# Squares' pieces in the rows' tiles, and norms spread by two transfers

## The chip, the cores and the metric

The kernel runs on one core of a Trainium2 chip. The metric is device time in microseconds of one execution, as the median of several runs. The core has a matrix engine (TensorE, PE in the profile; its weight loads are PEld), VectorE (DVE), ScalarE (ACT), GpSimd (POOL) and a queue engine (SyncE, SP) that issues nearly all transfers of this kernel, in one order.

## The reference

One layer of an encoder for two groups of tokens, 1024 of `x_sample` and 256 of `x_prompt`, 2048 features each:

```
hn   = rms_norm(x, norm_g)                      # x / sqrt(mean(x^2) + eps) * g
proj = hn @ w_in
...                                             # a state space part, a windowed attention,
...                                             # and an attention over 256 memory rows
mk, mv = split(rms_norm(mem, mem_norm_g) @ w_mem_kv)
return x + concat([o_ssd, o_att, o_mem]) @ w_out
```

What matters here is `rms_norm(x)`: for each of the 1280 tokens one number, 1/sqrt(mean of squares + eps), by which all 2048 features of that token are multiplied.

## The kernel before

**Products.** All large products are in float32, each operand split into a high half and a low half (`wh`, `wl` of the weights, `xH`, `xL` of the rows), and computed as three passes: high by high, high by low, low by high (lines 254 to 256, 289 to 291, 1199 to 1201). A weight tile is loaded into `wraw` (four buffers), ScalarE rounds it to `wh`, and VectorE subtracts to get `wl` (three buffers each; `wsplit`, lines 202 and 203). A block runs over 16 rounds, one for each 128 input features; a round has three passes for each of its four or five token tiles. Some weights are multiplied by a scheme of seven products for four (`block_pair`, `seven`), whose row sums lie in tiles tagged `tH0` to `tH7` and `tL0` to `tL7` of the pool `fin`.

**Order.** The 1280 tokens are ten tiles of 128: group 0 has tiles 0 to 4, group 1 tiles 5 to 9. The program begins with the two blocks of the memory rows (`mk`, then `mv`, four token tiles each), which need no norms of `x`. Then come the q block of group 0, ten units of the seven products, the blocks kv, mq, z0 and z1 of group 0, and then group 1. Beside the blocks run two lanes of small steps, written as generators: every round of a block advances each lane by a given number of steps (`pump`, with rates such as `MR[0]` = 1.75 for lane 0 in the memory blocks, from round 8 of the first). A step's instructions on ScalarE and VectorE are held behind the weight split that was traced last (`marks`). Within such limits a scheduler puts each engine's instructions in order by priority and by when it takes their inputs and buffers to be free, so a load may be issued long before the place where it is traced.

**Squares and norms.** `x_stats(0)` is in lane 0 beside the memory blocks. It takes the five token tiles of group 0 in twenty pieces of 128 x 512. A piece (`xst`) is loaded four steps ahead, ScalarE squares it and adds up its rows (line 1336), after four pieces VectorE adds the four sums, and GpSimd makes the power -1/2 (lines 120 and 121). The result is one column of `rx` per token tile: a number for each token, one token per partition. The pieces lie in the tiles tagged `evt` and `evu` of the pool `ev`, two buffers each, in which the tiles of the blocks' results (`mkr`, line 415) also lie. `x_stats(1)` does the same for tiles 8 and 9 beside the kv block, in other tiles; tiles 5 to 7 are done in between (`stage_stats`).

**Spreading the norms.** The rows are held with features on the partitions and tokens along the row, so the norms are needed along the row, the same on all 128 partitions: `rbc`, 128 x 640. `x_rows(grp)` makes it. It multiplies a broadcast column of `rx` by the identity, which gives a tile with the column turned into each of 128 rows, five times, into the PSUM tile `prx`, and VectorE copies the result to `rbc` (lines 1392 to 1397). In the profile each of the five products appears as two passes. The readers of `rbc` are `p_fill` (line 1234), which makes the rows of group 0 from round 9 of the `mv` block on, and `fill_direct` with `norm=True` (line 190), which makes those of group 1. The step of round 9 first asks that `x_rows(0)` be finished.

Of the kernel before, what the change touches and what calls it, by code (L numbers as in the profile page):

```python
# [10 lines left out]
F32 = mybir.dt.float32  # L11
# [8 lines left out]
P = 128  # L20
# [23 lines left out]
def hymba_encoder_kernel(  # L44
# [7 lines left out]
    V, A, G, T, S = nc.vector, nc.scalar, nc.gpsimd, nc.tensor, nc.sync  # L52
# [3 lines left out]
    def xrow(t):  # L56
        return x_sample[t * P:(t + 1) * P] if t < NS else x_prompt[(t - NS) * P:(t - NS + 1) * P]
# [8 lines left out]
    ev = ctx.enter_context(tc.tile_pool(name="ev", bufs=2))  # L66
# [4 lines left out]
    fin = early.enter_context(tc.tile_pool(name="early", bufs=1))  # L71
# [4 lines left out]
    def const(shape, name, dtype=F32):  # L76
        return cp.tile(shape, dtype, tag=name, name=name)
# [4 lines left out]
    def psum(name):  # L82
        return mix.tile([P, 512], F32, tag="mix", name=name)
# [3 lines left out]
    ident = identr.bitcast(F32)  # L87
# [11 lines left out]
    rx = const([P, 14], "rx")  # L99
    rbc = const([P, 640], "rbc")  # L100
    carry = const([P, 12, 4], "carry")
    def dram(shape, name):
        return dr.tile(shape, F32, tag=name, name=name)
# [8 lines left out]
    yp_d = [dram([P, 1024], f"yp_{t}") for t in range(NT)]  # L112
    sb_d = [dram([P, 1024], f"sb_{t}") for t in range(NT)]
    mk_d = dram([P, 4, 256], "mk_d")
    ac_d = [dram([160, P], f"ac_{g}") for g in range(2)]
    mr_d = [dram([P, 512], f"mr_{i}") for i in range(4)]
    mv_d = dram([P, 4, 512], "mv_d")
# [1142 lines left out]
    def p_step(j):  # L1260
        if j == 9:
            need(x_rows, [0])
        with ExitStack() as st:
            for ins in marks:
                st.enter_context(tc.issue_after(ins))
            if j in (25, 27):
                weight_sums(w_in_pairs, (j - 25) // 2)
            for f, k in sorted(p_plan.get(j, ()), key=lambda x: ((p_split, p_sums, p_fill, p_load).index(x[0]), x[1])):
                f(k)
# [53 lines left out]
    def stats(tiles, place, ahead=4, group=None):  # L1323

        n = 4 * len(tiles)
        group = group or n
        pieces, s4 = {}, None
        for g in range(0, n, group):
            m = min(group, n - g)
            for i in range(m + ahead):  # L1330
                if i >= ahead:
                    t, c = divmod(g + i - ahead, 4)
                    if c == 0:
                        s4 = sm.tile([P, 4], F32, tag="s4", name="xs4", bufs=4)
                    x = pieces.pop(g + i - ahead)
                    A.activation(x, x, AF.Square, accum_out=s4[:, c:c + 1])
                    if c == 3:
                        r = rx[:, tiles[t][1]:tiles[t][1] + 1]
                        V.reduce_sum(out=r, in_=s4, axis=AX.X)
                        rsqrt(r, r, 1.0 / D, 1)  # L1340
                if i < m:
                    t, c = divmod(g + i, 4)
                    pieces[g + i] = place(i)
                    with tc.issue_after(last_load[0].ins):
                        S.dma_start(pieces[g + i], tiles[t][0][:, c * 512:c * 512 + 512])
                yield

    def x_stats(grp):
        if grp == 0:
            yield from stats([(xrow(t), t) for t in range(5)],  # L1350
                             lambda i: ev.tile([P, 512], F32, tag="evt" if i % 2 else "evu", name="xst"))
        else:
            yield from stats([(xrow(t), t) for t in (8, 9)],
                             lambda i: mp.tile([P, 512], F32, tag="xs" if i % 2 else "ya", name="xst", bufs=2))
# [33 lines left out]
    def x_rows(grp):  # L1388

        yield  # L1390
        yield
        for o, n in ((0, 4), (4, 1)):
            ps = psum("prx")
            for i in range(n):
                t = 5 * grp + o + i
                T.matmul(ps[:, i * P:(i + 1) * P], rx[:, t:t + 1].broadcast_to([P, P]), ident, start=True, stop=True)
            V.tensor_copy(rbc[:, o * P:(o + n) * P], ps[:, :n * P])
        yield

    def refill_x(grp):  # L1400
        def f(q):
            need(x_rows, [grp])
            return [part(fill_direct, q, j, x_turned[grp, (4 * q + j) * P:(4 * q + j + 1) * P, :],
                         gain=vec[:, R_G + 4 * q + j:R_G + 4 * q + j + 1], norm=True) for j in range(4)]
        return f
# [60 lines left out]
    w_mk = w_mem_rows(0)  # L1466
    pend.extend(first[1:] + [u for q in range(1, 4) for u in refill_mem(q)])
    queue(0, x_stats, [0])
    queue(0, x_rows, [0])
    run(block_tok(w_mk, 4, ev_mk, places=TURNED), MR[0], hold=8)  # L1470
    V.tensor_scalar(out=vec[:, R_CB:], in0=vec[:, R_CB:], scalar1=0.5, scalar2=None, op0=ALU.mult)
# [54 lines left out]
    queue(0, mk_prep, range(4))  # L1526
    queue(0, mem_values, [0])
    queue(1, x_stats, [1])
    queue(1, x_rows, [1])
    w_kv = w_in_rows("kv")  # L1530
# [57 lines left out]
    for c in range(2, 4):  # L1588
        j0 = 16 * (c - 3)
        for k in block_tok(w_out_rows(c), 5, ev_out(c * 512), before_last=lambda _: beside_step(j0 + 14)):  # L1590
            if j0 + k == -7:
# [5 lines left out]
                fin = ctx.enter_context(tc.tile_pool(name="fin", bufs=2))  # L1597
# [83 lines left out]
```

## Time and profile before

| | us |
|---|---|
| Median of 3 runs (1801.31 to 1802.7) | 1802.39 |
| The profiled execution's time | 1802.42 |
| Its span, first to last instruction | 1800.7 |
| TensorE busy | 1791.2 (99%) |
| VectorE busy | 1244.3 (69%) |
| ScalarE busy | 903.0 (50%) |
| GpSimd busy | 439.5 (24%) |
| Granted TensorE clock | 1.000 |

Busy time of TensorE is the union of its passes. Passes overlap in the records, so the distance between the starts of two passes tells more than their length. A row of a stretch in order of time gives start, length, engine, line, operation, tiles, shape and count; in brackets stands the idle time before it and what ended it. A row of waits gives who waited for whom: total us, times, longest.

### The profile page before, as it was taken

To read this page: it belongs to the slowest core of one execution; us is meant where nothing else is said; L and a number is where in the kernel's file an instruction comes from. 1 tells how busy PE (TensorE), PEld (TensorE's weight loads), DVE (VectorE), ACT (ScalarE), POOL (GpSimd) and SP (SyncE) were. 2 spreads that over 40 slices of the span, in tenths; PEclk is the share of its full clock that TensorE was granted. 3 is DMA by queue.
4 is the path that set the end of the run, shared out by engine and by line. 5 is a ranking of instruction groups with operands and counts; after the bars stand their busy time and mean duration, and the time that the engine had idled before them with its cause. 6 is when DMAs were issued, how large, how long until landed. Compare 5 with 4: busy or idle time off the path is not lost.

```text
span 1800.7 us, 30423 instructions
## 1 busy us (share of the span) xinstructions
PE 1791.2 (99%) x10546; PEld 1606.1 (89%) x10546; DVE 1244.3 (69%) x2422; ACT 903.0 (50%) x2039; POOL 439.5 (24%) x714
## 2 busy tenths in 40 slices
PE   9999999999999999999999999999999999999999
PEld 7789999999887899999989987887898888889999
DVE  5595788877657978775755866666885654866665
ACT  6554455444445756564435646544574533543332
POOL 0105789961110000000000000001100000058775
PEclk9999999999999999999999999999999999999999
DMA  8664455446544644444436355457785564644442
GB/s 291 198 179 120 138 153 146 129 136 218 164 136 147 184 134 140 121 132 134 119 96 192 110 161 180 128 178 235 231 266 168 184 190 138 216 153 147 142 143 80
DMA packets 198891, 290.58 MB, mean 161 GB/s; under 512 B 18960, under 2 KB 80464, under 8 KB 198736
## 3 DMA queue, kind: packets, MB, share of 16 engines
q1 hardware_dynamic: 198592, 288.57, 52.7%
q8 instruction: 83, 1.36, 0.3%
q14 instruction: 72, 0.59, 0.1%
q10 hardware_dynamic: 144, 0.06, 0.0%
HBM read 231.12 MB, written 57.44 MB: 160 GB/s over the span
## 4 chain that ended last, share of the span: by engine, by line
PE 61%; DVE 1%; ACT 1%; issue 1%; DMA 1%; POOL 0%; POOLq 0%; ACTq 0%; DVEq 0%
PE acc L254 9%; PE acc L256 8%; PE acc L255 8%; PE acc L289 5%; PE acc L291 5%; PE acc L290 5%; PE acc L1199 3%; PE acc L1201 3%; PE acc L1200 3%; PE py L931 2%; PE po L674 1%; PE ppt L664 1%; PE accm L1200 1%; PE accm L1201 1%; PE accm L1199 1%
## 5 line engine op out<-in xcount | busy, mean ns | idle before, releaser
L203 DVE TENSOR_TENSOR wl<-wraw,wh 128x512 fp32r<-128x512 f32 (+1 forms) x480 | 338.9, 708 | 241.3 <-ACT wh L202 230.7
L254 PE MATMUL acc<-wh,xH 128*128 128x512 f32 (+1 forms) x1248 | 481.9, 386 | 0.2 <-ACT mkr L416 0.2
L255 PE MATMUL acc<-wl,xH 128*128 128x512 f32 (+1 forms) x1248 | 472.2, 378 | 0.9 <-DVE wl L203 0.6
L256 PE MATMUL acc<-wh,xL 128*128 128x512 f32 (+1 forms) x1248 | 472.8, 379 | 0.0
L202 ACT ACTIVATE wh<-wraw 128x512 fp32r<-128x512 f32 (+1 forms) x480 | 292.4, 613 | 323.5 <-PE acc L256 173.3
L254 PEld LDWEIGHTS acc<-wh,xH 128*128 128x128 f32 x1248 | 234.5, 188 | 45.1 <-issue 4.8
L255 PEld LDWEIGHTS acc<-wl,xH 128*128 128x128 f32 x1248 | 234.7, 188 | 43.8 <-DVE wl L203 3.3
L256 PEld LDWEIGHTS acc<-wh,xL 128*128 128x128 f32 x1248 | 234.2, 188 | 43.9 <-issue 0.9
L289 PE MATMUL acc<-xH,wh 128*128 128x320 f32 x640 | 204.5, 320 | 0.0
L291 PE MATMUL acc<-xH,wl 128*128 128x320 f32 x640 | 198.6, 310 | 0.0
L290 PE MATMUL acc<-xL,wh 128*128 128x320 f32 x640 | 198.3, 310 | 0.0
L203 DVE TENSOR_TENSOR sl<-ws,sh 128x384 fp32r<-128x384 f32 x144 | 99.6, 695 | 96.9 <-ACT sh L202 96.6
L202 ACT ACTIVATE sh<-ws 128x384 fp32r<-128x384 f32 x144 | 74.6, 523 | 176.5 <-POOL ws L1171 81.5
L1171 POOL TENSOR_TENSOR ws<-wraw 128x128 f32<-128x128 f32 x144 | 91.1, 633 | 202.0 <-DMA wraw<-in_w_in_pairs_dram 83.6
L289 PEld LDWEIGHTS acc<-xH,wh 128*128 128x128 f32 x640 | 120.3, 188 | 4.1 <-issue 3.7
L290 PEld LDWEIGHTS acc<-xL,wh 128*128 128x128 f32 x640 | 120.3, 188 | 2.6 <-issue 2.2
L291 PEld LDWEIGHTS acc<-xH,wl 128*128 128x128 f32 x640 | 120.1, 188 | 0.7 <-issue 0.6
L1171 POOL TENSOR_TENSOR ws<-wraw,ws 128x128 f32<-128x128 f32 x144 | 93.5, 649 | 11.3
L358 DVE SCALAR_TENSOR_TENSOR c<-u,vec,c 128x638 f32<-128x638 f32 (+1 forms) x96 | 88.6, 926 | 10.0 <-ACT c L353 9.7
L1171 POOL TENSOR_TENSOR ws<-ws,wraw 128x128 f32<-128x128 f32 x144 | 94.2, 654 | 0.0
L120 POOL TENSOR_SCALAR qr<-qss 128x8 f32<-128x8 f32 x10 | 4.3, 428 | 366.6 <-DVE qss L598 366.6
L1171 POOL TENSOR_TENSOR wraw<-wraw 128x128 f32<-128x128 f32 x144 | 89.2, 620 | 11.1
(427 smaller groups left out, 3645.1 us busy)
## 6 DMA issues: line engine op xcount, KB each, us to landing
wraw<-in_w_in_laid_dram SPq DMA_DIRECT2D x208, 256.0 KB, 2.8
wraw<-in_w_in_pairs_dram SPq DMA_DIRECT2D x80, 256.0 KB, 2.8
wraw<-in_w_out_laid_dram SPq DMA_DIRECT2D x64, 256.0 KB, 3.5
wraw<-in_w_out_pairs_dram SPq DMA_DIRECT2D x64, 256.0 KB, 2.8
rf<-ac SPq DMA_DIRECT2D x40, 256.0 KB, 3.7
rb<-ac SPq DMA_DIRECT2D x40, 256.0 KB, 4.1
wraw<-in_w_mem_laid_dram SPq DMA_DIRECT2D x32, 256.0 KB, 4.8
xst<-in_x_sample_dram SPq DMA_DIRECT2D x20, 256.0 KB, 4.7
```

Source lines behind the costliest of these rows:

```text
L202: a = A.activation(h, raw, AF.Copy)
L203: b = V.tensor_sub(l, raw, h.bitcast(F32))
L254: T.matmul(ps[t][:, :n], sh, h[:, :n], start=(k_ == 0), stop=False)
L255: T.matmul(ps[t][:, :n], sh, l[:, :n], start=False, stop=False)
L256: T.matmul(ps[t][:, :n], sl, h[:, :n], start=False, stop=(k_ == KT - 1))
L289: T.matmul(o, sh, cur["H", q][:, m, c], start=(k == 0), stop=False)
L290: T.matmul(o, sh, cur["L", q][:, m, c], start=False, stop=False)
L291: T.matmul(o, sl, cur["H", q][:, m, c], start=False, stop=(k == KT - 1))
L358: V.scalar_tensor_tensor(out=c[0], in0=u[:, k:k + n], scalar=cw[k], in1=c[0], op0=ALU.mult, op1=ALU.add)
L1171: G.tensor_tensor(out=o, in0=x, in1=y, op=op)
L1199: T.matmul(ps[p], h, xh, start=(k_ == 0), stop=False)
L1200: T.matmul(ps[p], h, xl, start=False, stop=False)
```

## The change

Two edits. The pieces of `x_stats(0)` lie in the tiles `tH4` to `tH7` and `tL4` to `tL7` in turn, eight places in the place of four; these tiles take the seven products' rows later on. And `x_rows` stores the five columns of `rx` to a small DRAM tile of 5 x 128, turned, and reads it back broadcast to all 128 partitions into `rbc`; the ten small products and the four copies are gone. The generator has five stops instead of three.

```diff
@@ -112,6 +112,7 @@
     mk_d = dram([P, 4, 256], "mk_d")
+    rx_d = [dram([5, P], f"rx_{g}") for g in range(2)]
     ac_d = [dram([160, P], f"ac_{g}") for g in range(2)]
@@ -1348,7 +1349,7 @@
     def x_stats(grp):
         if grp == 0:
             yield from stats([(xrow(t), t) for t in range(5)],
-                             lambda i: ev.tile([P, 512], F32, tag="evt" if i % 2 else "evu", name="xst"))
+                             lambda i: fin.tile([P, 512], F32, tag="tH tL".split()[i % 2] + str(4 + i // 2 % 4), name="xst"))
@@ -1389,12 +1390,10 @@
         yield
         yield
-        for o, n in ((0, 4), (4, 1)):
-            ps = psum("prx")
-            for i in range(n):
-                t = 5 * grp + o + i
-                T.matmul(ps[:, i * P:(i + 1) * P], rx[:, t:t + 1].broadcast_to([P, P]), ident, start=True, stop=True)
-            V.tensor_copy(rbc[:, o * P:(o + n) * P], ps[:, :n * P])
+        S.dma_start(rx_d[grp].rearrange("t p -> p t"), rx[:, 5 * grp:5 * grp + 5])
+        yield
+        S.dma_start(rbc, rx_d[grp].rearrange("t p -> (t p)").partition_broadcast(P))
+        yield
         yield
```

## The prediction

> **What bounds the kernel now.** I read the head of the page first, then the waits of the matrix engine, then the stretch from 20 to 150 us in which the changed lines of the first group run, engine by engine in order of time, and last the same lines of the second group around 446 us.
>
> ```profile
> span 1800.7 us, 30423 instructions
> PE 1791.2 (99%) x10546; PEld 1606.1 (89%) x10546; DVE 1244.3 (69%) x2422; ACT 903.0 (50%) x2039; POOL 439.5 (24%) x714
> ```
>
> TensorE is busy for 99% of the span. A change can win only in two ways: by taking passes off TensorE, or by closing one of its few gaps. Work taken off VectorE, ScalarE or a queue counts only where one of them makes TensorE wait. In the part that is touched (from the end of the first block, 45 us, into the second) these are its waits:
>
> ```profile
> PEld acc L255 <- DVE wl L203: 2.2, 4, 0.5
> PEld acc L254 <- ACT mkr L416: 0.6, 1, 0.6
> PEld acc L254 <- ACT wh L202: 0.5, 2, 0.2
> ```
>
> Columns: total us, times, longest. Four times the low half of a weight tile (wl) came late. The first and the last of the four, in order of time on TensorE:
>
> ```profile
> 58.13 0.39 PE L254 MATMUL acc<-wh,xH 128*128 128x512 f32 x1
> 58.63 0.50 PE L255 MATMUL acc<-wl,xH 128*128 128x512 f32 x1
> 58.97 0.40 PE L256 MATMUL acc<-wh,xL 128*128 128x512 f32 x1
> ...
> 67.87 0.46 PE L254 MATMUL acc<-wh,xH 128*128 128x512 f32 x1
> 68.55 0.50 PE L255 MATMUL acc<-wl,xH 128*128 128x512 f32 x1 [0.22 <-DVE wl L203]
> ...
> 73.24 0.39 PE L254 MATMUL acc<-wh,xH 128*128 128x512 f32 x1
> 73.47 0.39 PE L255 MATMUL acc<-wl,xH 128*128 128x512 f32 x1
> 73.69 0.39 PE L256 MATMUL acc<-wh,xL 128*128 128x512 f32 x1
> ```
>
> The last three rows show undisturbed 512-wide passes: they start 0.227 us apart on the mean (12 such passes a round of the weights here are 2.72 us). At 58.13 the distances are 0.50 and 0.34, so 0.39 us is lost; at 67.87 it is 0.68, with a second step of 0.11 as before: 0.57. The two between (61.3 and 64.5) lose 0.47 and 0.59. Together 2.0 us, close to the 2.2 of the waits' first row. Why is wl late? ScalarE and the load queue in the same stretch:
>
> ```profile
> 56.61 0.63 ACT L1336 ACTIVATE xst<-xst 128x512 f32<-128x512 f32 x1 [3.69 <-DMA xst<-in_x_sample_dram]
> ...
> 57.24 0.62 ACT L202 ACTIVATE wh<-wraw 128x512 fp32r<-128x512 f32 x1
> ...
> 52.51 1.01 SPq L1345 DMA_DIRECT2D xst<-in_x_sample_dram  x2
> ...
> 54.60 0.43 SPq L209 DMA_DIRECT2D wraw<-in_w_mem_laid_dram  x1
> ...
> 61.05 0.38 SPq L209 DMA_DIRECT2D wraw<-in_w_mem_laid_dram  x1
> ```
>
> ScalarE stood 3.69 us before the Square of a piece (xst) whose load was issued only at 52.51; the split wh queued behind that Square began at 57.24, and wl follows wh. The loads 52.51 to 61.05 are late because the pieces and the first block's evacuated tiles (mkr) share the same four places (two of evt, two of evu): the piece waits until mkr has been stored. After that each load waits for the Square four pieces back, and the weight load behind it waits too (one weight load at 54.60, the next at 61.05).
>
> **The change part by part.** First the products. Each group has five, seen as ten passes:
>
> ```profile
> L1396 PEld LDWEIGHTS prx<-identr,rx x20: 187/190/192, 73.7 to 446.1; 128*128 128x128 f32 x20
> ```
>
> In order of time on TensorE, the first group's:
>
> ```profile
> 73.92 1.28 PE L1396 MATMUL prx<-identr,rx 128*128 128x128 f32 x10
> 74.95 0.47 PE L254 MATMUL acc<-wh,xH 128*128 128x512 f32 x1
> 75.27 0.39 PE L255 MATMUL acc<-wl,xH 128*128 128x512 f32 x1
> ```
>
> From 73.92 to the next block pass at 74.95 are 1.03 us, and the pass behind them takes 0.32 instead of 0.227. So a group costs 1.1 us on a saturated engine, two groups 2.2 us. Nothing lies over it: that is the surest term, **-2.2 us**. The four copies to rbc on VectorE go as well:
>
> ```profile
> 75.39 0.88 DVE L1397 COPY rbc<-prx 128x512 f32<-128x512 f32 x2
> 76.31 0.89 DVE L1234 SCALAR_TENSOR_TENSOR ra<-ra,vec,rbc 128x640 f32<-128x640 f32 x1
> ```
>
> They are worth 0.9 us of VectorE per group and nothing in the sum, because TensorE does not wait for VectorE at that moment.
>
> Next the places. Eight of the tH/tL tiles (k of 4 to 7) hold a piece each. Their own first writer, p_split of k = 4, is traced 17 rounds of weights after the last Square, so sharing costs them nothing. A load now waits for the Square eight pieces back instead of four, and never for mkr. The ten loads that today leave from 52.5 us on can leave before 50. A Square is still held behind the weight splits traced before it: the twentieth belongs to step 24 of its lane. At 1.75 steps a round, from round 8 of the first block, that is round 5 of the second. That round's split needs round 2's buffer (three buffers): 3 x 12 x 0.227 us after about 50 us, or 58 us. Today the last Square ends here:
>
> ```profile
> 68.93 0.63 ACT L1336 ACTIVATE xst<-xst 128x512 f32<-128x512 f32 x1 [0.54 <-DMA xst<-in_x_sample_dram]
> ...
> 70.21 0.55 POOL L121 TENSOR_TENSOR rx<-rx,mhalf 128x1 f32<-128x1 f32 x1
> ```
>
> So the norms can be ready some 9 us earlier, and with data in hand ScalarE runs each Square and its readout in 0.7 us without standing in front of wh. I take the four waits as gone: **-2.0 us**. Bounds: -2.0 and 0 (they stay, or move). What could be late next is the evacuation wait of 0.6 us (mkr at 49.8). Its cause is another one:
>
> ```profile
> 49.40 0.53 ACT L202 ACTIVATE sh<-ws 128x384 fp32r<-128x384 f32 x1 [3.95 <-POOL ws L1171]
> 49.83 1.55 ACT L416 ACTIVATE mkr<-acc 128x512 f32<-128x512 f32 x3
> ```
>
> ScalarE stands 3.95 us for GpSimd's sums of an early weight tile, and the change does not touch that. I leave it at 0, with -0.5 as the far end.
>
> Then the two transfers. No row shows a 4-byte-per-row store or this broadcast. Nearest are:
>
> ```profile
> k<-kraw SPq DMA_DIRECT2D x10, 64.0 KB, 2.4
> rf<-ac SPq DMA_DIRECT2D x40, 256.0 KB, 3.7
> ```
>
> (us to landing, whole span), and from 23 to 46 us, when the queues are full:
>
> ```profile
> xst<-in_x_sample_dram SPq DMA_DIRECT2D x10, 256.0 KB, 5.2
> wraw<-in_w_mem_laid_dram SPq DMA_DIRECT2D x10, 256.0 KB, 5.5
> ra<-in_x_turned_dram SPq DMA_DIRECT2D x2, 320.0 KB, 5.1
> ```
>
> With two issues of 0.4 us the pair takes 6.9 us at the low end and 11.8 at the high one. From today's distance between the last Square's start and the ready norms (1.8 us) I get rbc at 58 + 1.8 + 6.9 = 67 to 72 us, against 76.3 today. The first reader, p_fill of k = 0, is traced in round 9, whose split needs round 6's buffer: 50 + 7 x 2.72 = 69 us. If VectorE stands there, the wl of round 10 is queued behind it; TensorE wants that at 50 + 10 x 2.72 = 77 us, and two fills, a difference and the split itself take 3 us. So rbc may come until about 74 us free of charge, and each us after that costs one. I take 0; the bound is a loss of 0 to 2 us.
>
> [...]
>
> On the queue, the read must wait for the store to land, with weight loads behind it. In both blocks four raw and three split tiles stand ahead of TensorE; two split tiles alone are 5.4 us (12 passes a round) in the first group and 6.8 us (15 passes) in the second, and the store's landing is 2.4 to 5.5. In the second group:
>
> ```profile
> 429.07 0.56 POOL L121 TENSOR_TENSOR rx<-rx,mhalf 128x1 f32<-128x1 f32 x1
> ...
> 447.95 0.88 DVE L190 SCALAR_TENSOR_TENSOR chd<-chd,vec,rbc 128x640 f32<-128x640 f32 x1
> ```
>
> The norms are ready at 429.6 and rbc is first read at 447.95, so 18 us are there for 7 to 12. Cost 0. The extra two steps per group leave the first lane exactly at the demand of round 9: 14 + 17.5 = 31 whole steps, and 25 + 6 are wanted. In the second group all of lane 1 (dt_prep, ssd_up) comes two steps later, a little over a round. It changes which small product falls beside which load; I put ±1.5 us on it, about the largest total that TensorE loses to one cause outside the start:
>
> ```profile
> PE pmt L759 <- DVE mpr L751: 1.3, 2, 0.8
> ```
>
> Last, fills that start 5 us earlier relieve VectorE in the q block, busy 46.8 of 54 us there, where two waits of TensorE on wl remain:
>
> ```profile
> 94.00:148.00 54.00, 53.89 (x237) 43.99 (x236) 46.83 (x77) 27.00 (x43) 8.13 (x13) 1.00 0.53 157
> ```
>
> (columns: span, then PE, PEld, DVE, ACT, POOL busy)
>
> ```profile
> PEld acc L255 <- DVE wl L203: 1.0, 2, 0.5
> ```
>
> Far end -1.0 us, taken 0.
>
> **Sum.** The profiled execution took 1802.42 us (1.7 around the span), the median of three is 1802.39. 1802.4 - 2.2 - 2.0 = **1798.2 us**.
>
> **The rivals.** A, the forecast. B: the places do not help. The queue, not the place, may hold the pieces, or ScalarE may now stand before earlier Squares; only the products go: 1802.4 - 2.2 = 1800.2. For it: in this stretch the DMA engines are nearly full.
>
> ```profile
> DMA packets 3860, 7.33 MB, mean 319 GB/s; under 512 B 427, under 2 KB 427, under 8 KB 3856
> ...
> q1 hardware_dynamic: 3856, 7.29, 92.9%
> ```
>
> (23 to 46 us; the last number is the share of 16 engines.) Against it: four loads of the same stretch (the two of ra and two more of the same kind, rb, 320 KB each) are not wanted before 70 us and can give way.
>
> C, slower: that same fullness decides. Ten pieces (2.62 MB) move from after 50 us into this stretch. At 319 GB/s they need 8.2 us; 7% idle gives 1.6, and the four loads that can give way 4.1. If nothing gives way and the pieces stand ahead of the weights in the one queue, weights come up to 8.2 - 1.6 = 6.6 us late. The split lead is no sure cover: ScalarE's two stands of 3.95 and 3.69 us already use up its 5.4, as the four waits show. Paid in full, this gives 1802.4 - 2.2 + 6.6 = 1806.8. It decides from a delay of 2.2 us that TensorE sees. Against it: up to 45 us the lead is whole, and loads of weights traced earlier go first.
>
> D: Squares end as late as today and the two transfers come on top: rbc at 70.8 + 6.9 to 11.8 = 78 to 83 us. With the four waits still there TensorE is 2 us later, so rbc is free until 76 us, and 2 to 7 us are paid. By the lower end, whose rows lie outside the full stretch: 1802.4 - 2.2 + 2 = 1802.2.
>
> **How the numbers follow.** A 0.52, B 0.33, C 0.10, D 0.05. 0.2% is 3.6 us, about what a measurement of this kernel can tell. A lies in part at the border (1798.8): 0.50 of it counts as faster. B, most of D and the weak ends of A and C are within 0.2%: 0.40. Slower: 0.10. A's own range is 1795.5 (both far ends, 1.5, and 1.2 of the reshuffle) to 1799.7. The range for 8 in 10 takes in B and D and leaves out C's strong end: 1795.5 to 1803.5.
>
> **What would show it.** Right: no prx rows; no wait of TensorE on wl between 55 and 70 us; last Square of the first group before 62 us; first fill before 74. Wrong: ScalarE standing for xst with wh behind it, weight loads landing over 8 us between 23 and 46, or the fills' reader waiting for rbc while wl is due.

## The result, and the profile after

The changed kernel takes 1815.89 us (median of 5 runs, 1815.71 to 1816.92) against 1802.39 for the kernel before beside it: 1.0073 times the time, 95% interval 1.0062 to 1.0084. It is 13.5 us slower, where 1798.2 was forecast, and lies outside the range of 1795.5 to 1803.5. The profiled execution took 1816.92 us. Its head:

```profile
span 1815.2 us, 30354 instructions
PE 1793.8 (99%) x10526; PEld 1608.0 (89%) x10526; DVE 1244.7 (69%) x2418; ACT 900.9 (50%) x2039; POOL 436.1 (24%) x714
```

The twenty passes are gone, yet TensorE is "busy" for 2.6 us more and stands for 11.9 us more (1815.2 - 1793.8 = 21.4, against 9.5 before). Its waits, total, times and longest:

```profile
PE acc L256 <- DVE wl L204: 5.6, 4, 3.6
PE psc L633 <- DVE lg L635: 2.0, 1, 2.0
PE acc L255 <- ACT wh L203: 1.7, 1, 1.7
PE pst L859 <- DVE bl L901: 1.6, 1, 1.6
```

Three of these four are new; the wait on wl had 0.6 us in the same list before. To see when they are paid, take three instructions that both traces have: the first evacuation of the mv block (`mvo`, at 93.0 us before), one in group 0's z blocks (`zs`, at 628.2), and the last difference of the rows (`yr`, 1797.4). In the changed kernel they start 0.4, 7.8 and 14.4 us later. These three offsets are used below for every kernel; each is of one profiled execution, against the one of before. Executions of one kernel lie up to 11 us apart (kernel 7: 1811.74 to 1823.06), mostly 1 to 7, so a difference of 1 or 2 us between two late offsets tells little.

**The first group.** SP, the queue engine (start, length):

```profile
60.51 0.39 SPq L1393 DMA_DIRECT2D rx<-rx  x1
61.66 0.34 SPq L210 DMA_DIRECT2D wraw<-in_w_mem_laid_dram  x1
70.80 0.33 SPq L1395 DMA_DIRECT2D rbc<-rx  x1
71.22 1.33 SPq L210 DMA_DIRECT2D wraw<-in_w_mem_laid_dram  x3
```

The norms go out at 60.5, as forecast. The read of them goes out 10.3 us later: SP stands for the store's landing (8.7 us by the waits of its queue), with three weight loads behind the read. VectorE:

```profile
69.07 0.69 DVE L204 TENSOR_TENSOR wl<-wraw,wh 128x512 fp32r<-128x512 f32 x1 [2.03 <-ACT wh L203]
75.99 0.88 DVE L1235 SCALAR_TENSOR_TENSOR ra<-ra,vec,rbc 128x640 f32<-128x640 f32 x1 [6.23 <-DMA rbc<-rx]
```

It stands 6.23 us for the read. The next wl (78.42) is queued behind the first fills, and on ScalarE the next wh (77.55) behind the rounding of the first filled rows (`xH`, 76.91), so that both splits come late. TensorE, in order of time:

```profile
76.14 0.39 PE L257 MATMUL acc<-wh,xL 128*128 128x512 f32 x1
78.22 0.50 PE L255 MATMUL acc<-wh,xH 128*128 128x512 f32 x1 [1.69 <-ACT wh L203]
79.16 0.50 PE L256 MATMUL acc<-wl,xH 128*128 128x512 f32 x1 [0.44 <-DVE wl L204]
...
80.46 0.63 PE L257 MATMUL acc<-wh,xL 128*128 128x512 f32 x1
80.89 0.63 PE L255 MATMUL acc<-wh,xH 128*128 128x512 f32 x1
```

From 76.14 to 78.22 a pass takes 2.08 us where 0.227 is usual here, and from 80 us on passes start 0.43 us apart: TensorE runs at half speed, with a granted clock of 0.51. The table by stretches shows where (us, busy PE, PEld, DVE, ACT, POOL, then the granted clock):

```profile
76.40:79.80 3.40, 1.27 (x5) 0.75 (x5) 3.39 (x6) 2.40 (x4) 0.00 (x0) 1.00 0.23 89
79.80:83.20 3.40, 3.40 (x10) 2.61 (x9) 3.26 (x8) 1.61 (x3) 0.00 (x0) 0.51 0.44 101
...
144.70:148.10 3.40, 1.81 (x7) 0.95 (x6) 3.37 (x6) 0.63 (x1) 1.81 (x3) 1.00 0.23 42
148.10:151.50 3.40, 3.40 (x9) 2.64 (x9) 0.04 (x1) 1.10 (x3) 2.25 (x6) 0.50 0.83 266
...
448.50:451.90 3.40, 0.98 (x5) 0.48 (x3) 1.97 (x3) 1.34 (x3) 0.00 (x0) 1.00 0.98 361
451.90:455.30 3.40, 2.24 (x5) 1.82 (x6) 3.13 (x6) 0.23 (x1) 1.53 (x2) 0.50 0.56 180
455.30:458.70 3.40, 3.40 (x9) 2.64 (x8) 3.31 (x7) 0.62 (x2) 0.30 (x2) 0.50 0.66 241
```

Three times a stretch of 3.4 us in which TensorE was busy for 1.8 us or less is followed by one at half the clock, and the third time the slow stretch, itself not full (2.24), by a second: four stretches, 13.6 us, on paper 6.8 us of time. The granted clock is 0.50 from 79.8 to 83.3, from 148.1 to 151.5 and from 451.9 to 458.7 us, so the half-speed periods last 3.4, 3.4 and 6.8 us; the table is cut close to where they begin and end. In the profile before the clock is 1.00 throughout. The gaps just ahead of them are 1.69 and 0.44 us at 76 us, 1.30 and 0.28 at 145, and one of 3.57 at 449, which reaches into the slow stretch. No run here gives a sure threshold: in kernel 9 below, the stretch from 143.3 us has a gap of 1.89 us and 1.55 us of busy time, and the clock stays at 1.00 behind it.

**The second group.** SP, ScalarE and VectorE:

```profile
434.23 0.38 SPq L1393 DMA_DIRECT2D rx<-rx  x1
434.71 0.51 SPq L210 DMA_DIRECT2D wraw<-in_w_in_laid_dram  x1
436.48 0.79 SPq L332 DMA_DIRECT2D k<-kraw  x2
444.10 0.32 SPq L1395 DMA_DIRECT2D rbc<-rx  x1
```
```profile
447.48 0.63 ACT L203 ACTIVATE wh<-wraw 128x512 fp32r<-128x512 f32 x1 [8.00 <-DMA wraw<-in_w_in_laid_dram]
```
```profile
449.93 2.48 DVE L191 SCALAR_TENSOR_TENSOR chd<-chd,vec,rbc 128x640 f32<-128x640 f32 x3 [9.72 <-DMA rbc<-rx]
```

Here a second thing shows. ScalarE stood 8.0 us for a weight tile whose load (434.71) was issued right behind the store: it landed only near 447, 12.7 us after its issue, against 7.9 for the slowest weight load of before. The k tiles stored beside it took up to 11.1 us (tile view, min/median/max: first the changed kernel, then the one before):

```profile
DMA to landing us min/median/max: 2.5/3.2/11.1
```
```profile
DMA to landing us min/median/max: 1.5/2.4/3.7
```

In the first group it is the same: the weight tile issued at 61.66 landed after 12.0 us. The slowest weight tile takes 12.5 to 13.1 us in the kernels below that have the same store (2, 6, 7, 11 and 12); in those with another form of it (3, 5, 8, 9, 10 and 13) no weight tile takes over 8.3 us and no k tile over 4.1. So where the store is slow its neighbours land late too, in kernels 6 and 7 even k tiles issued up to 2 us ahead of it (up to 10.7 and 12.2 us); why, no run here shows.

### The profile page after: what moved, and what is told of

Same layout as the page of the kernel before. It is cut to its first block, busy times and chain, and to the rows that moved or that the text cites. A ratio compares the mean times of both kernels' runs of the same rounds, so it can differ in the third digit from the quotient of the medians.

```text
span 1815.2 us, 30354 instructions
## 1 busy us (share of the span) xinstructions
PE 1793.8 (99%) x10526; PEld 1608.0 (89%) x10526; DVE 1244.7 (69%) x2418; ACT 900.9 (50%) x2039; POOL 436.1 (24%) x714
## 4 chain that ended last, share of the span: by engine, by line
PE 83%; issue 5%; POOL 4%; DMA 3%; DVE 3%; ACT 2%; SPq 0%; POOLq 0%; DVEq 0%; ACTq 0%
PE acc L255 13%; PE acc L256 13%; PE acc L257 13%; PE acc L1202 4%; PE acc L1200 4%; PE acc L1201 4%; PE acc L290 4%; PE acc L291 4%; PE acc L292 4%; POOL ws L1172 3%; PE py L932 2%; PE accm L1201 2%; PE accm L1202 2%; PE accm L1200 2%; PE po L675 1%
## 5 line engine op out<-in xcount | busy, mean ns | idle before, releaser
L359 DVE SCALAR_TENSOR_TENSOR c<-u,vec,c 128x638 f32<-128x638 f32 (+1 forms) x96 | 88.7, 927 | 11.9 <-ACT c L354 11.3
L1172 POOL TENSOR_TENSOR ws<-wraw,ws 128x128 f32<-128x128 f32 x144 | 93.9, 652 | 11.3
L1172 POOL TENSOR_TENSOR wraw<-wraw 128x128 f32<-128x128 f32 x144 | 87.9, 611 | 11.1
```

Source lines behind the costliest of these rows:

```text
L1172: G.tensor_tensor(out=o, in0=x, in1=y, op=op)
```

## The experiments

In short diffs, `-` is the line of the kernel named. "Before" is the kernel before, run beside each: medians 1803.71 (first four), 1803.11 (next four), 1802.55 (next three) and 1803.31 (last three).

**1. The places alone** (before with the new tiles for the pieces; products kept).

```diff
-  lambda i: ev.tile([P, 512], F32, tag="evt" if i % 2 else "evu", name="xst"))
+  lambda i: fin.tile([P, 512], F32, tag="tH tL".split()[i % 2] + str(4 + i // 2 % 4), name="xst"))
```

> The pieces alone move to the eight tH/tL tiles; the products stay. Theory 1 (the two transfers and the stands of VectorE and the load queue behind them make the whole loss): the four waits on wl between 58 and 68 us are gone, no wait over 1 us before 150 us, clock 1.000, about 1800.4 us (1802.4 - 2.0). Theory 2 (the crowded first stretch, rival C, makes the loss): weight loads late, TensorE waits between 40 and 75 us, 1806 us or more.

Measured: 1801.79 us (10 runs), ratio 0.9992 (0.9982 to 1.0001). Offsets -2.2, -1.2, +0.2: the four waits on wl are gone, as forecast, and 2.2 us are won by 93 us; in the profiled execution they are lost again by the end in four waits of about 1 us (600, 799, 1349 and 1374 us). The medians are 1.9 us apart, at the edge of what can be told (the interval reaches 1.0001). The pieces do not crowd the weights out.

**2. The transfers alone** (the changed kernel with the pieces in `evt` and `evu`).

> The transfers alone; the pieces stay in evt and evu. Theory 1: the norms are ready at about 71 us as in the kernel before, the store takes 10 us and the read 5, so VectorE stands until about 86 us with wl behind it; TensorE runs out near 80 us for 5 us or more, the clock is halved for some us after it, and group 1 stands as in the changed kernel: 1820 us or more. Theory 2: without the early pieces the transfers cost little, 1800 to 1803 us.

Measured: 1824.79 us (4 runs), ratio 1.0117 (1.0102 to 1.0133); offsets +11.1, +15.3, +22.9. With the Squares late, the read goes out at 81.3 and TensorE has a gap of 9.3 us. The loss is in the second edit, and the first one softens it.

**3. The store as 128 rows of 20 bytes.**

```diff
-    rx_d = [dram([5, P], f"rx_{g}") for g in range(2)]
+    rx_d = [dram([P, 5], f"rx_{g}") for g in range(2)]
-        S.dma_start(rx_d[grp].rearrange("t p -> p t"), rx[:, 5 * grp:5 * grp + 5])
+        S.dma_start(rx_d[grp], rx[:, 5 * grp:5 * grp + 5])
-        S.dma_start(rbc, rx_d[grp].rearrange("t p -> (t p)").partition_broadcast(P))
+        S.dma_start(rbc, rx_d[grp].rearrange("p t -> (p t)").partition_broadcast(P))
```

> As the changed kernel, but the store writes 128 rows of 20 bytes in place of 640 pieces of 4 bytes, and the read takes the same 2560 bytes as they lie, so the norms reach the tokens in another order than the reference's; the work is the same. Theory 1a (the number of pieces of 4 bytes makes the store slow): the store lands in 2.5 to 4 us, TensorE does not stand at 76 and 449 us, clock 1.000, 1798 to 1803 us. Theory 1b (any small store to DRAM that is waited for takes this long): 10 us as before and 1816 us.

Measured: 1803.95 us (10 runs), ratio 1.0006 (0.9996 to 1.0016); offsets -4.3, -6.4, -0.1. The norms reach the tokens in another order than the reference's here (and in kernel 10), so this kernel serves for its time alone. The store lands in 1.8 and 2.9 us instead of 10.3 and 9.9, both stands go, and TensorE is 6.4 us ahead at 628 us. SP and VectorE in the first group, to be put beside those of the changed kernel:

```profile
60.32 0.33 SPq L1393 DMA_DIRECT2D rx<-rx  x1
...
62.17 0.33 SPq L1395 DMA_DIRECT2D rbc<-rx  x1
```
```profile
69.49 0.88 DVE L1235 SCALAR_TENSOR_TENSOR ra<-ra,vec,rbc 128x640 f32<-128x640 f32 x1
```

This is the cleanest of the comparisons. In the two traces every engine runs the same instructions in the same order (but for three pairs of VectorE records that start within 0.1 us of each other), so only the form of the store and of its read differs: 14.2 us at 628 us (-6.4 against +7.8), 14.5 at the end, and 13.3 in the medians, each against the before beside it (13.5 and 0.2 us over it). Then, after 628 us, nearly all of the 6.4 us is lost. The largest piece, with its stretches:

```profile
710.07 0.44 PE L633 MATMUL psc<-kT,qT 128*128 128x384 f32 x1 [1.76 <-DVE lg L635]
```
```profile
707.30:710.70 3.40, 1.64 (x11) 1.38 (x10) 3.40 (x7) 2.32 (x6) 0.00 (x0) 1.00 0.57 148
710.70:714.10 3.40, 3.40 (x15) 3.40 (x15) 3.40 (x9) 0.00 (x0) 0.00 (x0) 0.50 0.06 6
```

So there are two losses, and the landing is one of them; this second one stands in both kernels.

**4. The store by itself.** The kernel before with eight small stores put beside the z0 and z1 blocks; one run, 1827.26 us. From 480 to 625 us other transfers landed late in it, `q` after 11.3 us and `za` after 8.8 (medians; 3.5 for both in the kernel before).

```diff
+    turned(5, "turna")                                              # 640 pieces of 4 bytes, side by side
+    probe(dram([P, 5], "rows20"), vec[:, :5])                       # 128 of 20
+    probe(dram([P, 5, P], "apart")[:, :, 0:1], vec[:, :5].unsqueeze(2))   # 640 of 4, each 512 from the next
+    turned(1, "turnone")                                            # 128 of 4
+    turned(2, "turntwo")                                            # 256 of 4
+    probe(dram([5, P], "rows512"), ident[:5, :])                    # 5 of 512
...
```

> The kernel before, with eight stores of a constant to DRAM tiles of their own beside the blocks z0 and z1, for which nothing waits; looked at is the time from issue to landing. 640 pieces of 4 bytes turned into 5 rows of 512 bytes (twice), 128, 256 and 1280 pieces of the same kind, 640 pieces each 512 bytes from the next, 128 rows of 20 bytes, 5 rows of 512 bytes. Theory 1a (number of pieces): 640 pieces 5 to 10 us wherever they go, 128 about 3, 256 about 4, 1280 about 15; 20-byte rows about 3 and 512-byte rows about 2. Theory 1c (pieces that go to the same small stretch of DRAM follow one another, so the place counts and not the number): 640 apart about 3 us, turned 640 5 to 10. The whole time should be 1802 to 1804 us.

Measured, us to landing (view of the DMA issues):

```profile
rows<-vec SPq DMA_DIRECT2D x1, 2.5 KB, 4.1
turnone<-vec SPq DMA_DIRECT2D x1, 0.5 KB, 9.2
...
turnten<-vec SPq DMA_DIRECT2D x1, 5.0 KB, 13.2
turnb<-vec SPq DMA_DIRECT2D x1, 2.5 KB, 11.7
```

The first turned store took 14.4. For the store apart and the five rows of 512 bytes the view gives no landing; from their issues (510.90 and 562.61) to their last semaphore updates it is 3.0 and 1.75 us. Ten times as many pieces cost 4 us more (9.2 to 13.2), so their number explains little: 640 pieces of 4 bytes land in 3.0 us where they lie 512 bytes apart, and in 11.7 to 14.4 where they lie side by side. Each form was stored once, the turned 640 twice. What is slow is 4-byte pieces next to each other in DRAM; why, no run here shows.

**5. 20-byte rows in the right order, three stops.** VectorE reads `rbc` through a view that puts the norms in order, and the two added stops are taken out.

```diff
+    rbcv = rbc.rearrange("p (q t) -> p t q", t=5)
...
-  V.scalar_tensor_tensor(out=x, in0=x, scalar=vec[:, g_:g_ + 1], in1=rbc, op0=ALU.mult, op1=ALU.mult)
+  V.scalar_tensor_tensor(out=hv(x, 5), in0=hv(x, 5), scalar=vec[:, g_:g_ + 1], in1=rbcv, op0=ALU.mult, op1=ALU.mult)
```

> The 20-byte store of the earlier run, the fills read rbc through a view that puts the tokens in order again, and x_rows has three stops as before, so lane 1 is not moved. Theory 1: store 2.4 us, no stand. Where did that run's lead of 5 to 6 us at 490 to 630 us go? Theory 3 (lane 1 comes two steps later and makes new waits at 470 and 708 us): with three stops the waits of 1.2 and 1.9 us and the half clock at 710 are gone, 1797 to 1799 us. Theory 4 (any change of the early part is given back later, since the order after it is made anew): 1801 to 1804 us, with other waits.

Measured: 1811.73 us (5 runs), ratio 1.0051 (1.0038 to 1.0063); offsets -2.3, +9.8, +11.1. The view is a new cost. Its fills, and those of the changed kernel (min/median/max in ns):

```profile
L1236 DVE SCALAR_TENSOR_TENSOR ra<-ra,vec,rbc x8: 1439/1472/1666, 70.6 to 135.8; 128x640 f32<-128x640 f32 x8
```
```profile
L1235 DVE SCALAR_TENSOR_TENSOR ra<-ra,vec,rbc x8: 875/878/884, 76.0 to 133.7; 128x640 f32<-128x640 f32 x8
```

0.59 us more on each of 32 fills is 19 us of VectorE, in the first group in stretches where it is nearly full (17.85 of 18 us from 76 to 94 us in the kernel before). The run does not tell about the stops, but after 628 us it loses only 1.3.

**6. The changed kernel with three stops.**

```diff
         S.dma_start(rx_d[grp].rearrange("t p -> p t"), rx[:, 5 * grp:5 * grp + 5])
-        yield
         S.dma_start(rbc, rx_d[grp].rearrange("t p -> (t p)").partition_broadcast(P))
         yield
-        yield
```

> The changed kernel with its 4-byte store, but x_rows with three stops. Theory 3: the waits of 1.7 and 2.2 us at 705 and 724 us go, and 4 to 5 us of the 13.5 with them: about 1811 us. Theory 4: they stay or others come: 1814 to 1818 us. The stands at 76 and 449 us stay in both.

Measured: 1815.03 us (4 runs), ratio 1.0064 (1.005 to 1.0078); offsets +0.7, +12.8, +14.1. The sum hides a trade: after 628 us it loses 1.3 instead of 6.6, but before that 5 more. In group 1 three k stores now stand beside the slow one, and ScalarE waits for them:

```profile
443.39 0.28 ACT L331 ACTIVATE kraw<-acc 128x128 f32<-128x128 f32 x1 [7.31 <-DMA k<-kraw]
```

**7. Group 1's fills held back** behind the weight splits traced last (the changed kernel), so that VectorE does not stand for `rbc` with wl queued behind.

```diff
+            with ExitStack() as st:
+                for ins in marks:
+                    st.enter_context(tc.issue_after(ins))
-            V.scalar_tensor_tensor(out=ch, in0=ch, scalar=gain, in1=rbc, op0=ALU.mult, op1=ALU.mult)
+                V.scalar_tensor_tensor(out=ch, in0=ch, scalar=gain, in1=rbc, op0=ALU.mult, op1=ALU.mult)
```

> The changed kernel, but the fills of group 1 that read rbc are held behind the weight split traced last, so that VectorE does not take them up in the mq block. Theory 5 (VectorE's stand before rbc is what stops TensorE at 449 us): the wait of 3.7 us and the half clock after it (6.8 us at half speed, 3.4 us lost) go, about 1809 us. Theory 6 (the load queue's stand of 10 us behind the store is enough by itself): a wait of 2 us or more on wh or wl stays at about 449 us, 1813 to 1816 us.

Measured: 1818.8 us (4 runs), ratio 1.0075 (1.0056 to 1.0094); offsets +1.2, +14.0, +20.5. VectorE's wait for `rbc` in group 1 is gone (6.7 us in all are left, all in group 0). The gap of 3.7 us at 449 is gone too, and one of 9.3 stands at 434.7, where ScalarE waits for the k stores issued up to 2 us ahead of the slow one, which land after 10.9 to 12.2 us. Freeing VectorE doesn't help while the store's neighbours land so late.

**8. Group 0 alone** (20-byte rows with the view in group 0, products in group 1).

> Group 0 as in the changed kernel but with the 20-byte store and the view, group 1 with its products as before (three stops, no lane moved). Theory 3: the lead of 4 us at 93 us is kept but for the 1.1 us of the products: 1798 to 1800 us. Theory 4: 1801 to 1804 us.

Measured: 1807.55 us (8 runs), ratio 1.0026 (1.0016 to 1.0036); offsets -3.0, +5.2, +4.9. Ahead at 93 us, it loses 8 us while sixteen slow fills (1.47 us) run; after 628 us, with group 1 as it was, it loses nothing.

**9. The norms turned on TensorE first**, so that the store carries five rows of 512 bytes in the order wanted; five stops as in the changed kernel.

```diff
-        S.dma_start(rx_d[grp].rearrange("t p -> p t"), rx[:, 5 * grp:5 * grp + 5])
+        ps = psum("prx")
+        T.transpose(ps[:5, :P], rx[:, 5 * grp:5 * grp + 5], ident)
+        V.tensor_copy(rbc[:5, :P], ps[:5, :P])
+        S.dma_start(rx_d[grp], rbc[:5, :P])
```

> The changed kernel with one edit: TensorE turns the group's 128x5 norms into 5x128 before the store (one pass and one VectorE copy of 5x128 in each group), so that the store carries five rows of 512 bytes, in the order that the read wants; read, stops and places of the pieces as in the changed kernel. Theory A (the long landing of the 4-byte store is what costs): the store lands in about 1.8 us instead of 5.2 to 10.3 (five such rows took 1.75 in the probe), the norms stand in all partitions at 68 to 70 us, VectorE stands under 2 us in group 0 and under 3 in group 1, no half-speed period before 600 us, and the time is 1800 to 1805. Theory B (the two transfers cost by being on the way at all, through the read or the queue that they share, whatever the store's form): over 1809.

Measured: 1806.61 us (11 runs), ratio 1.0018 (1.0009 to 1.0027); offsets -3.2, -3.4, +5.5; clock 1.00. SP and VectorE in the first group:

```profile
72.37 0.34 SPq L1396 DMA_DIRECT2D rx<-rbc  x1
...
73.79 0.38 SPq L1398 DMA_DIRECT2D rbc<-rx  x1
```
```profile
75.49 0.69 DVE L204 TENSOR_TENSOR wl<-wraw,wh 128x512 fp32r<-128x512 f32 x1 [2.18 <-ACT wh L203]
77.02 0.89 DVE L1235 SCALAR_TENSOR_TENSOR ra<-ra,vec,rbc 128x640 f32<-128x640 f32 x1 [0.83 <-DMA rbc<-rx]
```

The read follows the store after 1.4 us instead of 10.3. At 628 us this kernel is 11.2 us ahead of the changed one (-3.4 against +7.8). Not the store's form alone differs, though: from 60 us on the scheduler has made another order, in which the store goes out 12 us later. And that tells something: the first fill starts at 77.02, a microsecond later than in the changed kernel (75.99), yet TensorE has no wait between 45 and 94 us. Here two weight splits (72.62 and 75.49) stand ahead of the fill on VectorE; in the changed kernel the fill is next behind the split of 69.07, and the following split stands behind it. By these two traces it is not the hour at which rbc comes that stops TensorE in the first group, but VectorE's stand of 6.2 us with due splits queued behind it. My range for the whole time failed, because the later 8.8 us are still lost.

**10. 20-byte rows, three stops, no view** (kernel 3 without the two stops).

> The kernel with the 20-byte rows (norms in another order), with the two stops taken out that the change adds, so that store and read go out in one step; VectorE reads the norms side by side, at 0.88 us a fill, where the earlier one with three stops read them with a stride. Theory 3 (what the 20-byte kernel loses again after 628 us comes of lane 1 standing two steps later): the gap at 708 and its half-speed period are gone and the time is 1797 to 1801. Theory 4 (the order made anew loses it in some other place, whatever the stops): 1802 to 1806, with a gap of 1 to 2 us somewhere after 600 us. Theory 7 (the two long times of the earlier kernels with the strided norms came of the stride, 0.59 us more on each of 16 fills a group): under 1806 either way.

Measured: 1801.04 us (11 runs), ratio 0.9989 (0.998 to 0.9998); offsets -3.8, -3.7, -2.5. Against kernel 3 only the stops differ (and the order made from them, from group 1 on): the gap at 708 and its slow stretch are gone, and 1.2 us are lost after 628 instead of 6.3.

**11 and 12. Passes in the stands.** The changed kernel with passes that nothing reads, put ahead of the three passes that waited longest; 16, 8 and 30 of them at first, then 8, 6 and 15.

```diff
...
+                    if count[0] == 104:
+                        idle_passes(16)
                     T.matmul(ps[t][:, :n], sh, h[:, :n], start=(k_ == 0), stop=False)
+                    if count[0] in (198, 308):
+                        idle_passes(8 if count[0] == 198 else 30)
```

> The changed kernel with passes that nothing reads put into TensorE's order ahead of the three passes that it waited for longest: 16 of 128x128 at 76 us, 8 at 145, 30 at 449, about 0.11 us each by the ten products of before, so about as long as the stands (1.85, 1.5 and 3.7 us). Everything else is unchanged. Theory K (the half clock follows from TensorE's standing still, and costs 6.8 us of the time by itself): no half-speed periods at 80, 148 and 452 us, the three gaps show no idle time, and the time is 1808 to 1811. Rival (the half clock has another cause, or the stands themselves are the whole loss): half-speed periods stay, 1815 to 1819.

> The changed kernel with passes that nothing reads in TensorE's order at the same three places as in the earlier kernel with such passes, now cut to the length that they had there (32 records in 3.73 us, so 0.23 us for one pass of 128x128, which is two records): 8 at 76 us (1.9 us), 6 at 145 (1.4), 15 at 449 (3.5). Theory K (the half clock follows from TensorE's standing still and costs 6.8 us by itself): no half-speed periods at 80, 148 and 452 us, 1808 to 1812; a new gap at 156 us, as the earlier one showed, would cost up to 6 more and stand in its own half-speed period. Rival (the stands are the whole loss): 1815 to 1819 without any half-speed period.

Measured: 1830.31 us (5 runs), ratio 1.014 (1.012 to 1.0161), and 1825.46 (4 runs), ratio 1.0116 (1.01 to 1.0132); offsets of the second +1.6, +11.3, +18.3. The first had twice the length that was meant. The second, at the same places as the rows above:

```profile
76.95 1.95 PE L236 MATMUL idle<-identr 128*128 128x128 f32 x16
79.28 0.50 PE L264 MATMUL acc<-wh,xH 128*128 128x512 f32 x1 [0.38 <-ACT wh L203]
```
```profile
76.00:82.00 6.00, 5.18 (x30) 4.16 (x30) 4.87 (x8) 2.54 (x5) 0.00 (x0) 1.00 0.50 170
82.00:94.00 12.00, 11.56 (x50) 8.90 (x49) 11.81 (x19) 6.96 (x11) 0.00 (x0) 1.00 0.51 151
```

No half clock at 80, 148 or 452 us: with the gaps filled it is gone (granted clock 1.00 from 76 to 94, from 144 to 150 and from 455 to 462 us), so in the changed kernel it follows from TensorE's standing. But the kernel became slower, not 6.8 us faster, so that half of the theory fell. Up to 94 us VectorE is busy 11.81 of 12 us (11.85 in the changed kernel), and the slow passes ran beside its work: from the first pass behind the stand to the first evacuation of mv are 15.1 us in the changed kernel, with its half clock (78.22 to 93.35), and 15.3 here without (79.28 to 94.60). Only in group 1 is a gain seen: from the 2620th to the 2635th pass 3.45 us instead of 5.80. And a new wait of 2.7 us for the q block's evacuation, with its own half-speed stretch, came at 157 us (granted clock 0.79 from there to 165 us). What the half clock cost in the changed kernel after the first group is therefore not settled by itself; it is inside the 14.2.

**13. The turned norms with three stops** (kernel 9 without the two stops).

> The kernel in which TensorE turns the norms and five rows of 512 bytes are stored, with the two stops that the change adds taken out: store and read go out in one step. Norms in the right order, fills of 0.88 us. Theory 3 (the two stops, by which lane 1 stands two steps later, cost the 6 to 9 us after 628 us): the wait for lg near 712 us is under 0.5 us, the offset of minus 2 to minus 4 us at 628 us stays to the end, and the time is 1797 to 1801. Theory 4 (any new order loses it): 1803 to 1808.

Measured: 1801.77 us (11 runs), ratio 0.9988 (0.9979 to 0.9997) (the lowest ratio of all); offsets -3.6, -1.7, -0.5. The wait for lg is gone and 1.2 us are lost after 628 us. The gain at 628 is smaller than expected (a wait of 1.5 us for wl at 142 us has come), so the time is 1.5 us under before, where 2 to 6 were expected.

**14. The kernel before with two more stops**, nothing else.

```diff
             V.tensor_copy(rbc[:, o * P:(o + n) * P], ps[:, :n * P])
         yield
+        yield
+        yield
```

> The kernel before with one edit: two more stops in the step that makes the norms' rows, behind the products, so that lane 1 stands two steps later in each group and nothing else changes. Theory 3 (the stops cost the later time by themselves): a wait of 1.5 to 2.2 us for lg near 706 us, which the kernel before doesn't have, and 1804 to 1810. Theory 4: 1801 to 1803.5, no such wait.

Measured: 1808.4 us (8 runs), ratio 1.0024 (1.0013 to 1.0034); offsets +1.1, -0.1, +7.5. Two empty stops cost 5.1 us by the medians (2.3 to 6.1 by the interval), nearly all after 628 us (waits of 628 to 830 us, this kernel, then before):

```profile
PE psc L632 <- DVE lg L634: 1.9, 1, 1.9
...
```
```profile
PE ppt L664 <- DVE lg L652: 0.5, 1, 0.5
...
```

VectorE and TensorE at that wait:

```profile
712.55 0.68 DVE L934 TENSOR_TENSOR sk<-xs,dco 128x512 f32<-128x512 f32 x1
713.15 0.73 DVE L919 COPY_PREDICATED rb<-upper,rf 128x512 f32<-128x512 uint32 x1
...
714.37 1.69 DVE L358 SCALAR_TENSOR_TENSOR c<-u,vec,c 128x646 f32<-128x646 f32 x2
715.97 1.48 DVE L634 SCALAR_TENSOR_TENSOR lg<-ndist,psc 128x384 f32<-128x384 bf16 x3
```
```profile
716.58 0.44 PE L632 MATMUL psc<-kT,qT 128*128 128x384 f32 x1 [1.85 <-DVE lg L634]
```

The scores of the attention (psc) were ready at 714; `lg`, which empties them, stands behind five instructions of the state space lane. Both are small steps; two stops more in lane 1 put them on top of each other. The same wait, 1.8 to 2.2 us, is in every kernel with five stops in group 1 (after, 2, 3, 7, 9, 11, 12, 14) and in none with three (before, 1, 5, 6, 8, 10, 13), where it is 0.3 at most.

## Why the prediction was wrong, point by point

**The sum that was measured.** Kernel 3 at 628 us gives what the products and the places win with a short store in the same order of instructions, -6.4. The changed store adds 14.2 (11.2 if kernel 9, with its other order, is taken). From 628 us to the end the changed kernel loses 6.6, where kernel 14, with nothing but the stops, loses 7.6. -6.4 + 14.2 + 6.6 = 14.4, the third offset. The sum closes by the way its terms are taken; kernel 14 bears the last one out by itself.

**Products, -2.2, and four waits, -2.0: right where they stand.** By 93 us the four waits and one group's products were to win 3.1; measured are 3.2 (kernel 9), 3.6 to 3.8 (13 and 10) and 4.3 (3). Forecast for both groups -4.2; measured at 628 us -3.4 with one turning pass a group left in (kernel 9), and -3.7 and -6.4 without (kernels 10 and 3). No wait on wl was left between 55 and 70 us, and the norms were ready at 60.5 us, as worked out. But a gain at 93 us is not one at the end: of 2.2 and 3.6 us kernels 1 and 13 keep nothing and 0.5 in their profiled executions (1.9 and 1.5 in the medians).

**The two transfers, 0, with a loss of 0 to 2 as the bound: the step that failed first.** I took the store from the rows of 64 KB and 256 KB, 2.4 to 5.5 us. It took 10.3 and 9.9. The read came out about at its upper bound (5.2 and 5.8 against 5.5). For the order that the changed kernel has, the limit was placed well: rbc was free until about 74 us by the prediction, it came at 76, and TensorE stood from 76.4 us. As a limit on rbc itself it does not hold, since in kernel 9 rbc came a microsecond later and cost nothing; it belongs to the split queued behind the fill. What the prediction gave as its last sign of being wrong, the fills' reader waiting for rbc while wl is due, is what happened. And past it the price was not one us for each: by 93 us the changed kernel stands 4.7 us behind kernel 3. In group 1, where I saw 18 us of room for 7 to 12, the pair took 15.7 us from its issue at 434.2, VectorE came to the fills 9.7 us before the read had landed, and the neighbours landed late. A slow store got no chance of its own among the rivals; the prediction's own terms leave it 7.9 to 9.7 us (74 - 59.8 - 0.8, less a read of 3.7 to 5.5), and 10.3 passes that. The probe shows that the number of 4-byte pieces does not give the time by itself: 640 of them, 512 bytes apart, took 3.0 us, and 128 side by side 9.2.

**The cover on the queue: half right.** SP stood 8.7 us for the store in the first group, longer than the 5.4 us of split tiles, and 6.7 in the second, where they are 6.8. What I had not counted is that transfers issued ahead of the wait land late as well (12.0 and 12.7 us for a weight tile).

**The two stops, ±1.5: the step that failed second.** They cost 5.1 us by themselves in kernel 14; in the three pairs of kernels that differ in the stops (the changed one and 6, 3 and 10, 9 and 13) 1.6 to 5.6 us by the medians. The bound was taken from the largest loss to one cause in the trace before (1.3); the loss is several waits of 1 to 2 us and a slow stretch after one of them, none of which that trace holds.

**The rivals.** D had the nearest mechanism (rbc late) with the wrong reason (late Squares, which were on time) and a price of 2 where 14 were paid. C (crowding) fell with kernel 1, which also shows that the places do help early, against B.

## What to carry to other kernels

Store a column of numbers so that each row holds many bytes: turn it on chip first (5 rows of 512 bytes landed in 1.75 us), or let the reader take it in another order (128 rows of 20 bytes: 1.5 to 4.1 us), but don't scatter 4-byte pieces side by side (640 of them: 9.9 to 14.4 us); and don't let a strided operand into VectorE's full stretches in exchange (1472 ns a fill instead of 878). Look at what stands behind the reader of a transfer in its engine's order: a reader that is taken up too early stops whatever is due behind it, as VectorE's stand of 6.2 us did with the splits. Count a step's stops as a change of its own: try the kernel before with nothing but the new stops (here 5.1 us slower). Where TensorE is 99% busy, look at what every later stage does with the time won early, before adding gains up.

## What the runs showed of the hardware

- 4-byte pieces next to each other in DRAM (kernel 4 and the stores of the changed kernel): 9.2 us to landing for 128 of them, 9.9 to 14.4 for 640, 13.2 for 1280; 3.0 for 640 placed 512 bytes apart; 1.5 to 4.1 for 128 rows of 20 bytes; 1.75 for 5 of 512.
- Transfers issued beside such a store land late with it: a weight tile in each group 12.0 and 12.7 us, k tiles up to 11.1 (12.2 in kernel 7).
- Stretches of 3.4 us in which TensorE was busy for 0.98 to 1.81 us were followed by one at half the clock (three in the changed kernel), and one of 1.64 us in kernel 3; one of 1.55 us in kernel 9 was not. In the first group the slow passes cost nothing that is seen beside a VectorE busy for 11.8 of 12 us (15.1 us from the stand to the first evacuation with the half clock, 15.3 without).
- A VectorE operand of 128x640 read with a stride of five: 1472 ns instead of 878.
